# Two feed-forward layers: convolution biases and centre tap moved to ScalarE, five modulation vectors moved from TensorE to VectorE

## The chip, the cores and the metric

One core of one Trainium2 chip runs the whole program. The metric is the device time of one execution in microseconds; a kernel's time is the median of its runs. For the kernel before there are three runs: 2511.26, 2512.8 and 2514.46 us, median 2512.8 us. Engines are called as in the profile: PE is TensorE (PEld its weight loads), DVE is VectorE, ACT is ScalarE, POOL is GpSimd, SP is SyncE, whose queue issues the DMAs.

## The reference

Four transformer layers run one after the other on a latent stream `x` (512 tokens of 1024) and a context stream `ctx` (256 tokens): an attention layer with a feed-forward part (layer 0), an mLSTM layer with a feed-forward part (layer 1), and two gated mixing layers. Each layer is modulated by vectors that come from two conditioning inputs, `c` for the latents and `c_ctx` for the context. Cut to what the change touches:

```python
mod_lat = (jnp.dot(jax.nn.silu(c), ada_w[layer]) + ada_b[layer])[:, None, :]
mod_ctx = jnp.dot(jax.nn.silu(c_ctx), ada_w[layer]) + ada_b[layer]
sh1, sc1, gt1, sh2, sc2, gt2 = jnp.split(mod_lat, 6, axis=-1)
...
def dwconv(x, w, b):          # three taps along the tokens, zero padded at both ends of a stream
    ...
    return sum(xp[:, j:j + T] * w[j] for j in range(width)) + b

def conv_ffn(h, w_up, conv_w, conv_b, w_down):
    gate, val = jnp.split(jnp.dot(h, w_up), 2, axis=-1)
    return jnp.dot(jax.nn.silu(dwconv(gate, conv_w, conv_b)) * val, w_down)
```

In layer 1 the context is not updated any more after the mLSTM has read it, so `gt1`, `sc2`, `sh2` and `gt2` of layer 1 are needed for the latents alone, and so is the gate of the second mixing layer. The other vectors are needed for both streams.

## The kernel before, in words

Activations lie with channels on the partitions and tokens on the columns: 768 columns, context first (0 to 255), then latents (256 to 767). Two more columns, 768 and 769, carry the modulation shifts, so that a product's last two columns are the bias that each stream gets (latents, context). The normalisation factor of a token is applied after the product, as a row `h.r`.

Each fp32 product is made of three with the operands split into a high and a low part (`split`, line 355: ACT writes the high part, DVE the rest). Weights come by DMA from SP's queue into `raw` (three buffers) and are split into `wh` and `wl` (four half tiles each, `weight`, line 398) one weight ahead of the product that uses them. `lin` (line 407) issues a product into a PSUM tile from `A` (three of them in the feed-forward layers).

The work is one program order written by hand: `blk` (line 508) issues the splits for the next weight, the matmuls of a block, then `fill`, then `tick`, which runs what earlier blocks have put off with `later`; the evacuation of a block is so issued behind the matmuls of the next one. Every engine runs its own part of this order in sequence.

A feed-forward layer (`ffn`, line 896) goes through 22 groups of 128 hidden channels. A group has two products over eight tiles of inputs, gate and value, each 24 pairs of matmuls; in between the down products of earlier groups are issued (`plan_ffn`, line 875: chunks of 2, 2 and then six times 3 groups; for each of eight output tiles one product, evacuated by `add_x`, line 859). In layer 0 it covers both streams, in layer 1 the latents alone.

The gate's evacuation (`g1`, line 905) runs on DVE but for the two-column bias and the tanh: `put` (line 821) multiplies by `h.r` and adds the bias per stream, `conv` (line 842) makes the centre tap with the convolution's bias and then two taps per stream, `silu2` (line 852) the activation. The value's (`v1`, line 910) multiplies by the result and splits it for the down product.

Sixteen modulation vectors are made on the side (`modvec`, line 530). A vector takes eight steps. A step loads 128 rows of 1024 weights into an `ada` buffer (two of them, loads run two steps ahead) and issues four matmuls of 256 columns, one for each quarter of the columns (the profile counts each as two). After the last step ACT copies the result, PE transposes it twice, and DVE adds the bias (`turn`, line 550). `fill` (line 644) takes such steps off one list `todo`, in the order in which `run` (line 2332) put them there, as long as the `quota` of the stage lasts: 24 steps in the first layer's mixer, 48 in its feed-forward part, 24 in the second feed-forward part, 16 and again 16 in the first mixing layer. In a feed-forward layer `blk` takes one step per weight (two for groups 1 and 2), and the down products one for every second output tile. So the feed-forward part of layer 0 makes `gt2_0`, `sc1_1`, `sh1_1`, `gt1_1`, `sc2_1` and `sh2_1`; that of layer 1 `gt2_1`, `s_sc_0` and `s_sh_0`; `s_gt_1` comes last in the first mixing layer, two steps within its output products (line 2123) and six in the passage to the second (`fill(2)` in line 2153 and `pre`, line 2156).

Of the kernel before, what the change touches and what calls it, by code (L numbers as in the profile page):

```python
# [9 lines left out]
F32 = mybir.dt.float32  # L10
F32R = mybir.dt.float32r
BF16 = mybir.dt.bfloat16
AF = mybir.ActivationFunctionType
ALU = mybir.AluOpType
# [4 lines left out]
D = 1024  # L19
NL = 512  # L20
NC = 256
T = NL + NC
HALF = T // 2
W = 776
STATS = {0: (0,), 1: (1, 2), 2: (3, 4), 3: (5, 6), 4: (7,)}
CP = lambda j, qi, m: j == 1
KT = D // 128
FF = 2816
NFB = FF // 128
# [113 lines left out]
def _prepare(inp):  # L143

    a = {k: np.asarray(v) for k, v in inp.items()}
    o = dict(_constants())
    xt = np.concatenate([a["ctx"][0], a["x"][0]], 0).T
    o["xT"] = np.ascontiguousarray(xt.reshape(KT, 128, T))
    o["cT"] = np.ascontiguousarray(a["ctx_2"][0].T.reshape(KT, 128, NC))
    o["ada"] = a["ada_w"]  # L150
    o["mod"] = a["w_mod_2"]

    blk = lambda s, n: [np.arange(s + 128 * i, s + 128 * i + 128) for i in range(n)]
# [5 lines left out]
    for h in range(8):  # L159
        n, r = h * 96 + np.arange(64), h * 96 + 64 + np.arange(32)  # L160
# [19 lines left out]
    gt = np.concatenate([np.concatenate([g0 + s + np.arange(8), np.full(24, g0)]) for s in (0, 16, 8, 24)])  # L180
# [18 lines left out]
    cols, at = [], {}  # L199
# [30 lines left out]
    for n in ("gqa_q_g", "gqa_k_g"):  # L230
        g = a[n][0]
# [33 lines left out]
class _Kernel:  # L265


    def __init__(self, ctx, tc, I, at, out):
        self.tc, self.nc, self.I, self.at, self.out = tc, tc.nc, I, at, out
        pool = lambda name, bufs, **k: ctx.enter_context(tc.tile_pool(name=name, bufs=bufs, **k))  # L270
        self.kp = pool("k", 1)
        self.pa = pool("a", 36)
        self.pp = pool("pt", 3)
        self.pw = {n: pool(n, b) for n, b in (("raw", 3), ("ada", 2), ("wh", 4), ("wl", 4))}
        self.ps = pool("sm", 24)
        self.pr = pool("rm", 4)
        self.pm = pool("mo", 1)
        self.psa, self.banks = pool("psa", 2, space=PSUM), None
        self.dr = pool("dr", 1, space=DRAM)
        self.todo, self.due, self.mods, self.coming = [], [], {}, set()  # L280
        self.wq, self.wi, self.wraw, self.wsp = [], 0, {}, {}
        self.nraw = self.nspl = 0
        self.hook = self.mid = None
        self.quota, self.log = 0, False

    def split_psum(self, a, at=0):

# [229 lines left out]
    def cond(self, names, key):  # L517

        S = self.const("S" + key, [128, KT, 32])
        self.nc.vector.memset(S, 0.0)  # L520
        for v, n in enumerate(names):
            x = self.s(n, 0, KT)
            th = self.sm(8)
            self.act(th, x, AF.Tanh, scale=0.5)
            u = self.sm(8)
            self.ts(u, x, 0.5)
            self.stt(S[:, :, v], th, 1.0, u, ALU.add, ALU.mult)
        return S

    def modvec(self, name, S, w, c0, bias):  # L530
        nc = self.nc
# [319 lines left out]

    def silu2(self, x, c):

        th = self.a(name="th")
        self.act(th[:, c], x[:, c], AF.Tanh, scale=0.5)
        self.stt(x[:, c], th[:, c], 1.0, x[:, c], ALU.add, ALU.mult)
        return x
# [38 lines left out]
    def ffn(self, l, h, order, make_next):  # L896
        lat, c = h.lat, h.c
        segs = (SL,) if lat else (SL, SC)
        acts = {}
        nxt = None  # L900

        def gate(i):
            st = {}

            def g1(ps):
                g = self.put(ps, h)
                cv = self.conv(g, [self.s(f"fcw{l}{j}", i) for j in range(3)], self.s(f"fcb{l}", i), lat)
                st["s"] = self.silu2(cv, c)

            def v1(ps):  # L910
                v, cv = self.a(name="val"), st["s"]
                b = self.bias(ps)
                self.tt(v[:, c], ps[:, c], h.r[:, c])
                for s, (c0, c1) in enumerate(segs):
                    self.stt(v[:, c0:c1], v[:, c0:c1], b[:, s:s + 1], cv[:, c0:c1], ALU.add, ALU.mult)
                acts[i] = self.parts(v, c, "ah")
            seg = LATB if lat else ALLB
            if i == 0:
                self.begin([(f"w_up{l}", 0, seg, g1), (f"w_up{l}", 1, seg, v1)], h)
                return  # L920
            for j, evac in ((0, g1), (1, v1)):
                self.blk(f"w_up{l}", 2 * i + j, h.hs, seg, evac, 1 + (i < 3))

        def early(nxt):

            for k in range(KT):
                self.feed(nxt, k, True, (1,))
                if k:
                    yield
            self.sums(nxt, (1,))  # L930
            yield
            self.inverse(nxt, (1,))

        gt, gens = None, []
        step, _ = self.side(gens)
        for o in order:
            if o[0] == "up":
                gate(o[1])
                continue
            _, i, n, d0 = o  # L940
            last = i + n == NFB
            if gt is None:
                gt = self.half(f"gt2h_{l}", f"gt2_{l}")
            if last and not lat:
                self.tick()
                nxt = make_next()
            if lat and o is order[-2]:
                nxt = make_next()
                gens.append(early(nxt))
            xs = [acts.pop(j) for j in range(i, i + n)]  # L950
            b = WIDE[n]
            for m2 in range(D // b):
                w = self.weight(f"w_dn{l}", d0 + m2 * 128 * n * b)
                for e in range(b // 128):
                    ps = self.lin(w, xs, LAT if lat else ALL, off=128 * e, stride=b)
                    self.tick()
                    self.later(lambda m=b // 128 * m2 + e, ps=ps, n=nxt if last else None: self.add_x(m, ps, gt, lat, n))
                    step()
                    if e % 2:
                        self.fill(1)  # L960
        self.flush()
        return nxt

    def project(self, name, xs, segs, gt, lat, nxt):
# [1367 lines left out]
    def run(self):  # L2332
        nc, I = self.nc, self.I
# [8 lines left out]
        nc.vector.memset(self.eps, EPS)  # L2342
        S1 = self.cond(("c", "c_ctx"), "1")
        S2 = self.cond(("c_2", "c_ctx_2"), "2")
        for l in range(2):
            for j, n in ((1, "sc1"), (0, "sh1"), (2, "gt1"), (4, "sc2"), (3, "sh2"), (5, "gt2")):
                if l or j > 1:
                    self.modvec(f"{n}_{l}", S1, I["ada"][l], 1024 * j, self.s(f"ada_b{l}", 8 * j, 8))
        for l in range(2):
            for j, n in ((1, "s_sc"), (0, "s_sh"), (2, "s_gt")):  # L2350
                self.modvec(f"{n}_{l}", S2, I["mod"][l], 1024 * j, self.s(f"mod_b{l}", 8 * j, 8))
        self.plan_even()
        orders = [self.plan_ffn(0)]
        self.plan_odd()
# [29 lines left out]
        def norm(A, g, sc, sh, lat=False):  # L2384
            return lambda: self.start(self.gain(A, sc, g), self.mod(sh), lat)

        h = self.start(self.const("A_a0", [128, KT, 2]), self.const("m_sh1_0", [128, KT, 2]))
        pre = self.first_mods(S1, I["ada"][0], 1024, 0, self.s("ada_b0", 8, 8), self.s("ada_b0", 0, 8), self.s("n1g0", 0, KT), h, consts, after)
        self.quota = 24
        h = self.even(h, pre, norm("f0", self.s("n2g0", 0, KT), "sc2_0", "sh2_0"))  # L2390
        self.quota = 48
        h = self.ffn(0, h, orders[0], norm("a1", self.s("n1g1", 0, KT), "sc1_1", "sh1_1"))
        h = self.odd(h, norm("f1", self.s("n2g1", 0, KT), "sc2_1", "sh2_1", True))
        self.quota = 24
        h = self.ffn(1, h, orders[1], norm("s0", self.s("gpre0", 0, KT), "s_sc_0", "s_sh_0"))
        self.quota = 16
        h, pre, post = self.second(0, h, norm("s1", self.s("gpre1", 0, KT), "s_sc_1", "s_sh_1"))
# [25 lines left out]
```

## Time and profile before

| | before |
|---|---|
| median of 3 runs | 2512.8 us |
| the profiled execution's own time | 2511.48 us |
| its span in the trace | 2509.7 us |
| mean granted TensorE clock | 0.989 of full speed |
| PE busy | 2441.3 us, 97% |
| DVE busy | 1554.0 us, 62% |
| ACT busy | 962.2 us, 38% |
| POOL busy | 213.9 us, 9% |
| DMA | 234.99 MB, mean 94 GB/s |

The profiled execution took 1.8 us more than its span; this lies around the span and is taken as fixed. Busy shares are averages over stages: PE does most of the work nearly everywhere, and what a stage costs is read from the stage. A timeline line that ends in "xN" is N instructions of one kind in a row, its duration from the start of the first to the end of the last. The feed-forward part of layer 0 lies at about 507 to 1104 us of the span, that of layer 1 at about 1434 to 1813 us, the passage between the mixing layers at about 2203 to 2266 us.

### The profile page before, as it was taken

The page shows a single profiled execution, that of the slowest core. Times are in us where ns is not written, and L with a number is a line of the kernel's source. Part 1 is how long each engine was busy: PE and PEld are TensorE (multiplying, and loading weights), DVE is VectorE, ACT ScalarE, POOL GpSimd, SP SyncE. Part 2 cuts the span into 40 slices and gives each one's busy share as a digit, 9 for nine tenths or more (in the row PEclk, how much of TensorE's full clock was granted, in tenths as well). Part 3 has the DMA queues.
Part 4 walks back from the last instruction along what each step waited for, and adds up shares of the span by engine and source line. Part 5 has one row for each costly group of instructions (what it writes and reads, how often), then busy time and mean ns, then how long its engine had stood idle before and what let it go on. Part 6 is the DMA issues. An engine that isn't in the chain of part 4 may idle for free.

```text
span 2509.7 us, 40462 instructions
## 1 busy us (share of the span) xinstructions
PE 2441.3 (97%) x16296; PEld 2038.9 (81%) x16296; DVE 1554.0 (62%) x2780; ACT 962.2 (38%) x2203; POOL 213.9 (9%) x149
## 2 busy tenths in 40 slices
PE   7998999999999999998999999999999999999998
PEld 5776666887888888887889888999978778879797
DVE  4436876556555656668566566766755575267764
ACT  4226666322211222243445422233432374343563
POOL 2001232100000000022110100000010000130001
PEclk9999999999999999998999999999999999999999
DMA  8441110124343321113122255222223202332012
GB/s 286 152 153 46 32 65 29 61 91 143 117 128 126 110 84 68 55 64 110 60 64 68 93 175 178 97 97 93 85 82 121 90 1 69 102 118 78 18 47 88
DMA packets 81866, 234.99 MB, mean 94 GB/s; under 512 B 9936, under 2 KB 22288, under 8 KB 81680
## 3 DMA queue, kind: packets, MB, share of 16 engines
q1 hardware_dynamic: 81392, 232.36, 28.1%
q8 instruction: 128, 2.10, 0.3%
q14 instruction: 58, 0.48, 0.1%
q10 hardware_dynamic: 288, 0.07, 0.0%
HBM read 229.73 MB, written 2.66 MB: 93 GB/s over the span
## 4 chain that ended last, share of the span: by engine, by line
PE 86%; DVE 7%; ACT 3%; DMA 2%; issue 1%; SPq 0%; POOL 0%; DVEq 0%; ACTq 0%; POOLq 0%
PE A L353 69%; PE B L353 14%; PE B L1075 3%; DMA ada<-in_ada_dram 1%; DVE sm L1064 1%; DVE wl L344 1%; DVE kf L344 1%; DVE conv L341 1%; ACT P L332 0%; DVE hl L341 0%; DVE put L344 0%; ACT wh L332 0%; DMA stsel<-in_stat_dram 0%; ACT hh L332 0%; DVE y L344 0%
## 5 line engine op out<-in xcount | busy, mean ns | idle before, releaser
L353 PE MATMUL A<-hh,wh 128*128 128x258 f32 (+2 forms) x2704 | 648.0, 321 | 11.9 <-ACT wh L332 4.1
L353 PE MATMUL A<-hl,wh 128*128 128x258 f32 (+2 forms) x2704 | 631.9, 315 | 2.7 <-DVE hl L341 2.7
L353 PE MATMUL A<-hh,wl 128*128 128x258 f32 (+2 forms) x2704 | 631.5, 315 | 0.1
L344 DVE TENSOR_TENSOR wl<-raw,wh 128x512 fp32r<-128x512 f32 (+2 forms) x533 | 368.8, 714 | 414.3 <-ACT wh L332 400.7
L332 ACT ACTIVATE wh<-raw 128x512 fp32r<-128x512 f32 (+2 forms) x533 | 310.7, 603 | 566.7 <-PE A L353 398.5
L353 PEld LDWEIGHTS A<-hh,wh 128*128 128x128 f32 x2704 | 420.2, 191 | 73.7 <-issue 12.1
L353 PEld LDWEIGHTS A<-hl,wh 128*128 128x128 f32 x2704 | 420.0, 190 | 36.3 <-DVE hl L341 3.8
L353 PEld LDWEIGHTS A<-hh,wl 128*128 128x128 f32 x2704 | 420.1, 190 | 33.8 <-DVE wl L344 0.5
L344 POOL TENSOR_TENSOR sq<-sq 128x768 f32<-128x768 f32 (+2 forms) x45 | 65.5, 1457 | 1200.6 <-ACT sq L332 595.9
L332 ACT ACTIVATE P<-A,sm 128x768 f32<-128x768 f32 (+3 forms) x176 | 128.0, 727 | 96.9 <-DVE sm L1064 90.9
L353 PE MATMUL A<-ah,wh 128*128 128x512 f32 (+1 forms) x528 | 163.1, 363 | 1.2 <-DVE x L341 1.1
L353 PE MATMUL A<-ah,wl 128*128 128x512 f32 (+1 forms) x528 | 159.7, 357 | 0.0
L353 PE MATMUL A<-ahl,wh 128*128 128x512 f32 (+1 forms) x528 | 159.3, 356 | 0.0
L1064 DVE TENSOR_REDUCE sm<-A 128x1 f32<-128x768 f32 (+3 forms) x176 | 129.2, 735 | 44.4 <-PE A L353 43.6
L341 DVE SCALAR_TENSOR_TENSOR x<-A,gt2h,x 128x512 f32<-128x512 f32 x192 | 119.7, 656 | 43.3 <-PE A L353 43.2
L1075 PE MATMUL B<-ident,P 128*128 128x128 f32 x768 | 124.4, 286 | 7.7 <-DVE pt L1078 2.7
L1075 PEld LDWEIGHTS B<-ident,P 128*128 128x128 f32 x768 | 83.8, 143 | 51.2 <-issue 21.5
L332 ACT ACTIVATE th<-conv 128x768 f32<-128x768 f32 (+1 forms) x52 | 38.4, 738 | 223.1 <-DVE conv L341 223.1
L341 DVE SCALAR_TENSOR_TENSOR conv<-put,small,conv 128x511 f32<-128x511 f32 (+1 forms) x168 | 111.5, 678 | 5.0
L353 PEld LDWEIGHTS A<-ah,wh 128*128 128x128 f32 x528 | 86.8, 188 | 27.0 <-issue 4.6
L344 DVE TENSOR_TENSOR put<-A,rbc 128x768 f32<-128x768 f32 (+1 forms) x111 | 93.2, 840 | 21.4 <-ACT sm L332 21.4
L353 PE MATMUL B<-ada,S 128*32 128x256 f32 x1152 | 91.2, 397 | 8.7 <-DMA ada<-in_ada_dram 8.5
(369 smaller groups left out, 3301.1 us busy)
## 6 DMA issues: line engine op xcount, KB each, us to landing
raw<-in_w_up_dram SPq DMA_DIRECT2D x88, 512.0 KB, 3.3
raw<-in_w_in_dram SPq DMA_DIRECT2D x81, 512.0 KB, 4.5
ada<-in_ada_dram SPq DMA_DIRECT2D x80, 512.0 KB, 4.1
ada<-in_mod_dram SPq DMA_DIRECT2D x48, 512.0 KB, 3.8
raw<-in_w_dn_dram SPq DMA_DIRECT2D x48, 384.0 KB, 3.1
raw<-in_w_o_dram SPq DMA_DIRECT2D x24, 512.0 KB, 4.3
ada<-in_ada_dram SPq DMA_DIRECT2D x16, 384.0 KB, 8.0
raw<-in_w_dn_dram SPq DMA_DIRECT2D x8, 512.0 KB, 5.7
```

The source lines that it names most:

```text
L332: return self.nc.scalar.activation(out, in_, f, **k)
L341: return self.nc.vector.scalar_tensor_tensor(out, x, sc, y, op0=op0, op1=op1)
L344: return (e or self.nc.vector).tensor_tensor(out, x, y, op=op)
L353: return self.nc.tensor.matmul(out, l, r, start=start, stop=stop)
L1064: nc.vector.tensor_reduce(g.nm[:, z], u.ps[:, cols], axis=AX.X, op=ALU.max, negate=True)
L1075: nc.tensor.transpose(ps[:, 128 * i:128 * i + 128], u.P[:, c:c + 128], self.ident)
```

## The change

Three things are changed.

In the feed-forward gate the biases leave the streams. The gate is kept without its bias, in a buffer with one column of padding on either side of a stream; ACT writes minus the bias there, DVE multiplies PSUM by `h.r` once per stream, ACT makes the centre tap with a bias that stands for both (`bc`, one two-column DVE operation with the sum of the taps, `wsum`), and DVE adds the two outer taps in one operation each over both streams at once.

Five vectors, those needed for the latents alone, are made by `modrow` in place of `modvec`. Their weights come transposed (`lone`): a step loads a tile of 128 output channels by 1024 and multiplies it by the conditioning row, held on all partitions, with the sum as a second output of the same DVE instruction. The row is written to DRAM once for each of the two conditioning inputs and loaded by one DMA on all 128 partitions, once in each feed-forward layer.

The order of the list and one quota change: the feed-forward part of layer 0 now takes 56 steps (24 of `modvec`, then 32 of `modrow`), that of layer 1 two vectors of `modvec` and then `s_gt_1` by `modrow`.

```diff
@@ _prepare
+    o["lone"] = np.stack([w[:, 1024 * j:1024 * j + 1024].T.reshape(KT, 128, D)
+                          for w, j in [(a["ada_w"][1], j) for j in (2, 4, 3, 5)] + [(a["w_mod_2"][1], 2)]])
@@ _Kernel
+    def modrow(self, name, v, i, bias):
+        nc, st = self.nc, {}
+
+        def load(k):
+            st[k] = self.pw["ada"].tile([128, 1024], F32, tag="ada", name="ada")
+            nc.sync.dma_start(st[k], self.I["lone"][i, k])
+
+        def step(k):
+            if self.row is None or self.row[0] != v:
+                self.row = v, self.pt(n=D)
+                nc.sync.dma_start(self.row[1], self.sd[v:v + 1].to_broadcast([128, D]))
+            if k == 0:
+                st["m"] = self.const("m_" + name, [128, KT, 2])
+                nc.gpsimd.memset(st["m"], 0.0)
+            m, raw = st["m"], st.pop(k)
+            nc.vector.scalar_tensor_tensor(raw, raw, 1.0, self.row[1], op0=ALU.mult, op1=ALU.mult, accum_out=m[:, k, 0:1])
+            if k == KT - 1:
+                self.tt(m[:, :, 0], m[:, :, 0], bias, ALU.add)
+                self.mods[name] = m
+
+        for k in range(KT):
+            self.todo.append((lambda k=k: load(k), lambda k=k: step(k)))
@@ silu2
-        th = self.a(name="th")
+        th = self.a(n=W, name="th")
@@ ffn, gate
             def g1(ps):
-                g = self.put(ps, h)
-                cv = self.conv(g, [self.s(f"fcw{l}{j}", i) for j in range(3)], self.s(f"fcb{l}", i), lat)
-                st["s"] = self.silu2(cv, c)
+                w = [self.s(f"fcw{l}{j}", i) for j in range(3)]
+                g, d, bc = self.a(n=W, name="gate"), self.a(n=W, name="conv"), self.sm()
+                self.ts(bc, ps[:, T:T + 2], wsum[:, i:i + 1], self.s(f"fcb{l}", i), ALU.mult, ALU.add)
+                for v, ((c0, c1), z) in enumerate(zip(segs, at)):
+                    n = c1 - c0
+                    self.act(g[:, z - 1:z + n + 1:n + 1], ps[:, T + v:T + v + 1].to_broadcast([128, 2]), scale=-1.0)
+                for v, ((c0, c1), z) in enumerate(zip(segs, at)):
+                    n = c1 - c0
+                    self.tt(g[:, z:z + n], ps[:, c0:c1], h.r[:, c0:c1])
+                    z0 = z - 2 if len(segs) > v + 1 else z
+                    self.act(d[:, z0:z + n], g[:, z0:z + n], AF.Identity, scale=w[1], bias=bc[:, v:v + 1])
+                for j in (0, 2):
+                    self.stt(d[:, lo:hi], g[:, lo - 1 + j:hi - 1 + j], w[j], d[:, lo:hi])
+                st["s"] = self.silu2(d, slice(lo, hi))
...
+        wsum = self.const("wsum", [128, NFB])
+        self.tt(wsum, self.s(f"fcw{l}0", 0, NFB), self.s(f"fcw{l}1", 0, NFB), ALU.add)
+        self.tt(wsum, wsum, self.s(f"fcw{l}2", 0, NFB), ALU.add)
+
+        at = (NC,) if lat else (NC + 3, 1)
+        lo, hi = at[-1], at[0] + NL
...
         self.flush()
+        self.row = None
         return nxt
@@ run
+        for n, l, j in (("gt1", 0, 2), ("sc2", 0, 4), ("sh2", 0, 3), ("gt2", 0, 5), ("sc1", 1, 1), ("sh1", 1, 0)):
+            vec(n, l, j)
+        for i, (n, j) in enumerate((("gt1", 2), ("sc2", 4), ("sh2", 3), ("gt2", 5))):
+            self.modrow(n + "_1", 0, i, self.s("ada_b1", 8 * j, 8))
+        vec2("sc", 0, 1)
+        vec2("sh", 0, 0)
+        self.modrow("s_gt_1", 1, 4, self.s("mod_b1", 16, 8))
+        for n, l, j in (("gt", 0, 2), ("sc", 1, 1), ("sh", 1, 0)):
+            vec2(n, l, j)
+        self.sd = self.dr.tile([2, D], F32, tag="sd", name="sd")
...
         h = self.even(h, pre, norm("f0", self.s("n2g0", 0, KT), "sc2_0", "sh2_0"))
-        self.quota = 48
+        for v, S in enumerate((S1, S2)):
+            nc.sync.dma_start(self.sd[v].rearrange("(k p) -> p k", p=128), S[:, :, 0])
+        self.quota = 56
```

## Rows read from the trace of the kernel before

**Rows 1.** Page, part 1: busy us, share of the span, instructions.

```profile
PE 2441.3 (97%) x16296; PEld 2038.9 (81%) x16296; DVE 1554.0 (62%) x2780; ACT 962.2 (38%) x2203; POOL 213.9 (9%) x149
```

**Rows 2.** Busy time in stretches: PE, PEld, DVE, ACT, POOL, clock, DMA.

```profile
689.00:886.00 197.00, 197.00 (x1209) 160.27 (x1209) 111.31 (x185) 39.91 (x77) 0.00 (x0) 1.00 0.39 125
886.00:1083.00 197.00, 197.00 (x1125) 172.52 (x1125) 123.90 (x203) 44.05 (x86) 0.00 (x0) 1.00 0.19 64
...
1563.00:1813.00 250.00, 250.00 (x1763) 234.21 (x1765) 176.77 (x291) 81.48 (x182) 6.09 (x6) 1.00 0.28 93
```

**Rows 3.** Chain in order of time, layer 0 feed-forward, with steps: start, us, what.

```profile
652.15 8.62 PE A L353 x48
...
661.34 8.62 PE A L353 x48
...
688.92 0.37 PE B L553 x2
...
698.29 6.50 PE A L353 x36
...
705.36 6.50 PE A L353 x36
```

**Rows 4.** Timeline of PE, layer 0, no steps: two pairs, 24 pairs apart.

```profile
895.91 0.51 PE L353 MATMUL A<-hh,wh 128*128 128x512 f32 x2
...
904.33 0.51 PE L353 MATMUL A<-hh,wh 128*128 128x512 f32 x2
```

**Rows 5.** Chain in order of time, layer 1 feed-forward, with steps.

```profile
1537.61 5.93 PE A L353 x48
...
1544.11 5.93 PE A L353 x48
```

**Rows 6.** Timeline of PE, layer 1, no steps: two pairs, 24 pairs apart.

```profile
1659.75 0.41 PE L353 MATMUL A<-hl,wh 128*128 128x256 f32 x2
...
1665.50 0.41 PE L353 MATMUL A<-hl,wh 128*128 128x256 f32 x2
```

**Rows 7.** Timeline of PE and of DVE around the passage between the mixing layers.

```profile
2212.55 1.07 PE L353 MATMUL B<-ada,S 128*32 128x256 f32 x16
2213.55 1.16 PE L353 MATMUL B<-rm,ident 128*128 128x128 f32 x8
2217.60 0.79 PE L353 MATMUL A<-hh,wh 128*128 128x256 f32 x2 [2.89 <-ACT hh L332]
...
2211.82 0.29 DVE L341 SCALAR_TENSOR_TENSOR rm<-rm 128x128 f32<-128x128 f32 x1
```

**Rows 8.** Groups by shape: count, busy us, mean ns of one, idle before.

```profile
L341 DVE SCALAR_TENSOR_TENSOR conv<-th,conv 128x768 f32<-128x768 f32 x28 | 26.8, 957 | 21.8 <-ACT th L332 21.8
...
L332 ACT ACTIVATION_READ_ACCUMULATOR P<-A,sm 128x1 f32 x176 | 34.2, 194 | 0.0
```

**Rows 9.** Timeline of DVE, layer 1, no steps: a gate, then a value.

```profile
1666.08 0.69 DVE L344 TENSOR_TENSOR put<-A,rbc 128x512 f32<-128x512 f32 x1
...
1667.90 1.54 DVE L341 SCALAR_TENSOR_TENSOR conv<-put,small,conv 128x511 f32<-128x511 f32 x2
1670.14 0.69 DVE L341 SCALAR_TENSOR_TENSOR conv<-th,conv 128x512 f32<-128x512 f32 x1 [0.70 <-ACT th L332]
1670.75 1.16 DVE L344 TENSOR_TENSOR wl<-raw,wh 128x512 fp32r<-128x512 f32 x2
...
1674.60 0.74 DVE L341 SCALAR_TENSOR_TENSOR x<-A,gt2h,x 128x512 f32<-128x512 f32 x1
```

**Rows 10.** Timeline of DVE and of PE, layer 1, second set of down products.

```profile
1521.00 2.06 DVE L341 SCALAR_TENSOR_TENSOR x<-A,gt2h,x 128x512 f32<-128x512 f32 x3
...
1521.80 0.49 PE L353 MATMUL A<-ah,wh 128*128 128x512 f32 x1 [0.60 <-DVE x L341]
```

**Rows 11.** DMA issues: engine, count, KB each, median us to landing.

```profile
pt<-cb SPq DMA_DIRECT2D x16, 256.0 KB, 5.0
...
de<-de SPq DMA_DIRECT2D x4, 4.0 KB, 7.5
```

More of the change, by code (lines that the diff above doesn't have):

```diff
@@ L283, in __init__ @@
         self.hook = self.mid = None
-        self.quota, self.log = 0, False
+        self.quota, self.log, self.row = 0, False, None
     def split_psum(self, a, at=0):
@@ L913, in v1 @@
                 self.tt(v[:, c], ps[:, c], h.r[:, c])
-                for s, (c0, c1) in enumerate(segs):
-                    self.stt(v[:, c0:c1], v[:, c0:c1], b[:, s:s + 1], cv[:, c0:c1], ALU.add, ALU.mult)
+                for s, ((c0, c1), z) in enumerate(zip(segs, at)):
+                    self.stt(v[:, c0:c1], v[:, c0:c1], b[:, s:s + 1], cv[:, z:z + c1 - c0], ALU.add, ALU.mult)
                 acts[i] = self.parts(v, c, "ah")
@@ L2344, in run @@
         S2 = self.cond(("c_2", "c_ctx_2"), "2")
[L2345 to L2351, printed above, removed]
+        vec = lambda n, l, j: self.modvec(f"{n}_{l}", S1, I["ada"][l], 1024 * j, self.s(f"ada_b{l}", 8 * j, 8))
+        vec2 = lambda n, l, j: self.modvec(f"s_{n}_{l}", S2, I["mod"][l], 1024 * j, self.s(f"mod_b{l}", 8 * j, 8))
+        for n, l, j in (("gt1", 0, 2), ("sc2", 0, 4), ("sh2", 0, 3), ("gt2", 0, 5), ("sc1", 1, 1), ("sh1", 1, 0)):
[8 more added lines that the diff above has]
+        self.sd = self.dr.tile([2, D], F32, tag="sd", name="sd")
         self.plan_even()
```

## The prediction

> **What bounds the kernel now.** I read the page first: PE is busy 97% of the span, DVE 62%, ACT 38% [rows 1]. An average over stages proves little, so I went to the stretches in which the change acts. In the feed-forward part of layer 0, with modulation steps (689 to 886 us) and without them (886 to 1083 us), PE is busy all 197.00 of 197 us, and in that of layer 1 without steps 250.00 of 250 us [rows 2]. So nothing hides the steps there: each microsecond of PE taken out shortens the run, as long as DVE, which takes the work over, does not become late. DVE is busy 123.90 of 197 us (63%) in layer 0 and 176.77 of 250 us (71%) in layer 1 where no steps run [rows 2].
>
> **What one step costs PE.** A block of 24 matmul pairs starts every 661.34 - 652.15 = 9.19 us with a step in it [rows 3]; the same 24 pairs without one take 904.33 - 895.91 = 8.42 us [rows 4]. The step costs 0.77 us, more than its own matmuls' place in the chain, since the pairs at either side of it move apart. In the down products 18 pairs with a step take 705.36 - 698.29 = 7.07 us [rows 3] against 18/24 x 8.42 = 6.32 us: 0.75. I use 0.76. In layer 1 a block takes 1544.11 - 1537.61 = 6.50 us with a step [rows 5] and 1665.50 - 1659.75 = 5.75 us without [rows 6]: 0.75. The two transposes that end a vector take 0.37 us in the chain [rows 3], partly in place of the gap behind a step; I take 0.2.
>
> **Part 1: five vectors leave PE.** The list decides where. Layer 0's feed-forward part loses `gt1_1`, `sc2_1`, `sh2_1`: 24 x 0.76 + 3 x 0.2 = 18.8 us. Layer 1's loses one vector in sum (`gt2_1` has been made before, `s_gt_1` comes in as a row product): 8 x 0.75 + 0.2 = 6.2 us. In the first mixing layer the eight steps of `s_gt_1` go. Two lie among full products: 2 x 0.76 = 1.5 us. Two stand together at 2212.55 and hold up the products that spread the normalisation row by 2213.55 - 2212.55 = 1.0 us; DVE had finished that row at 2211.82 + 0.29 = 2212.11, so this 1.0 us is gained. The other four lie where PE waits anyway (2.89 us for ACT at the first product [rows 7]): nothing. With the transposes: 2.7 us. Together 27.7 us.
>
> **Part 2: forty row products arrive on DVE.** The trace has no such operation with a sum output. Its nearest rows are the same instruction with two SBUF inputs and no sum: 957 ns for 768 columns [rows 8] and 0.69 us for 512 [rows 9], so (957 - 690)/256 = 1.04 ns a column and 0.16 us fixed. For 1024 columns this gives 1.22 us, the low bound. A sum that is read out costs ACT 194 ns [rows 8]; I take 1.4 us, since the instruction itself is known and only the read-out is new. The high bound is two cycles for each column: 0.16 + 1024 x 2.08 ns + 0.19 = 2.5 us.
>
> Layer 0: a block takes PE 8.42 us. DVE's 63% of it is 5.3 us; a row product makes 6.7; DVE's existing waits for ACT (21.8 us over 28 activations [rows 8], twice in two blocks) add 0.8: 7.5 us. It fits, so this is costed at nothing under PE; if DVE ran 1 us over per block instead, 32 steps would cost up to 32 us.
>
> Layer 1 is tighter. In two blocks PE has 11.5 us; DVE's gate runs from 1666.08 to 1670.75 = 4.67 us, the splits and the value's evacuation to 1674.60 = 3.85 us, the other block's splits 1.2 us [rows 9]: 9.7 us. Two row products make 12.5 us, 1.0 us too much, for two groups only; `A` has three tiles and weights are split a block ahead, so an arrear of 2 us is carried. But four of the eight row products fall into down products with short blocks. There two output tiles take PE 12 x 5.75/24 = 2.9 us, and DVE 2 x 0.69 (three evacuations in 2.06 us [rows 10]) + half of 1.16 (a split pair serves four tiles [rows 9]) + 1.4 = 3.4 us. PE already waits 0.60 us for such an evacuation there [rows 10]. So I give these four steps back whole: -3.0 us. Bounds for layer 1: 6.2 us if the arrear is carried, -3 us if a late row load is added.
>
> **Part 3: the gate.** Per gate DVE loses the bias additions and the centre tap (in layer 1 between 1666.08 + 0.69 and 1667.90, 1.13 us [rows 9]) and in layer 0 two of four outer taps; it gains a two-column operation (0.2 us) and a wait for ACT's centre tap, which I size by the tanh of the same shape, 0.70 us of idle time [rows 9]. In layer 1 the gate stays at 4.67 - 1.13 + 0.2 + 0.7 = 4.4 us; in layer 0 it gets shorter, with two streams overlapping ACT and DVE. ACT's additions fall on an engine that is busy 81.48 of 250 us [rows 2]. Behind the waiting DVE stand the next weight's low parts, for which PE waits one block later. As PE does not wait for the gate now, part 3 gains and costs nothing; uncovered it could cost what the wait exceeds the margin of 11.5 - 9.7 = 1.8 us.
>
> **Part 4: queues.** The 40 weight loads replace 40 of the same 512 KB on SP's queue; their buffers are now freed by DVE. New are two scattered writes of 1024 runs of 4 bytes and two loads of a row onto 128 partitions. The nearest rows: four scattered loads of 256 runs each, together 1024 runs in flight, land in 7.5 us, and a 256 KB broadcast in 5.0 us [rows 11]. Two writes, about 15 us, stand in front of weight loads when two weights, 2 x 8.42 = 16.8 us of PE, are in hand: 0, at worst 15 if that cover failed. The broadcast keeps DVE waiting 0 to 5 us at the first row product of each layer, with evacuations and splits behind it; in layer 0 a block of slack covers it, in layer 1 it is in the bound above. I take 0.
>
> **Sum.** 18.8 + (6.2 - 3.0) + 2.7 = 24.7 us. The profiled execution, 2511.48 us (span 2509.7 and 1.8 around it), lies 1.3 us under the median of 2512.8; it becomes 2486.8, the median 2488.1. I forecast 2487.5 us, with 2482 to 2493 for this case alone. About 0.2% (5 us) is what a measurement of this kernel can tell from no change.
>
> **Rivals.** *Row products at half rate.* Each then takes 2.5 us. For it: a sum output is new here. Against it: without it the same instruction with two fp32 SBUF inputs runs at 1.04 ns a column, one a cycle like a plain product. In layer 0 a block would ask DVE for 5.3 + 2.5 + 0.8 = 8.6 us of 8.42: some 0.2 x 32 = 6 us, of which the shorter gate gives 1 to 2 back. In layer 1 eight times 1.1 us more, of which some 2 us are carried: 7 us. Time 2487.5 + 4.5 + 7 = 2499 us. Chance 0.16. [...]
>
> *The hand-over to ACT becomes the bound, and the kernel gets slower.* The place is the first outer tap of each of the 22 gates of layer 1, where DVE's queue stops until ACT has run the centre tap. With a wait of 0.7 us there are 1.8 us of margin and 0.3 gained; it loses once the wait passes 2.8 us, and at 3.9 us the loss, 22 x 1.1 = 24 us, cancels the gain. At 4.2 us: 22 x 1.4 = 31 us, 2487.5 + 31 = 2518.5 us. For it: ACT runs in order and splits weights too. Against: ACT idles two thirds of that stretch [rows 2] and the tanh hand-over costs 0.70 us. Chance 0.04.
>
> *The saving is eaten.* DVE's arrears in layer 0, or the scattered writes, take 15 to 25 us back: about 2508. Against it stands DVE's 63%. Chance 0.05.
>
> *More is gained.* The four steps in layer 1's down products come free too and the passage shortens further: 2487.5 - 3.0 - 2.5 = 2482 and below. Chance 0.09.
>
> **Chances and range.** The forecast case has 0.66. Faster by over 0.2% (under 2507.8): 0.66 + 0.16 + 0.09 = 0.91, less 0.02 for the eaten saving's doubtful edge: 0.89. Within 0.2%: 0.07. Slower: 0.04. The range of 2481 to 2500 takes in the forecast, half rate and most of the better case.
>
> **What would show it.** Right: in layer 0 blocks of 8.42 us from 689 us on with PE busy throughout; row products of about 1.4 us; layer 1's up blocks 5.75 us with row products beside them, while its second down products gain nothing; the passage's spread products about 1 us earlier. Wrong: row products of 2.5 us; waits of PE for `wl` or for evacuations in the stretches where it had none; idle time of DVE before the outer taps above 2.8 us; weight loads landing late at the start of layer 0's feed-forward part.

## The result and the profile after

The changed kernel takes 2487.23 us (median of 4 runs, 2485.67 to 2489.86) beside 2512.03 us for the kernel before (4 runs): ratio 0.9903, 95% interval 0.9892 to 0.9915. The forecast was 2487.5 us. The profiled execution took 2486.04 us, with a span of 2484.3 us, 25.4 us less than before.

The page's busy time by engine, after:

```profile
PE 2408.3 (97%) x15966; PEld 2027.6 (82%) x15966; DVE 1549.1 (62%) x2771; ACT 1010.7 (41%) x2286; POOL 215.9 (9%) x154
```

Against [rows 1], PE is 33 us less busy and ACT 48 us more. DVE stands where it was (1549.1 us for 1554.0): the gate gave up 45.5 us (e1, below) and forty row products take 51.8. The same stretches as in [rows 2] (columns: PE, PEld, DVE, ACT, POOL, granted clock, DMA share, GB/s):

```profile
689.00:886.00 197.00, 197.00 (x1124) 172.24 (x1123) 141.24 (x235) 53.65 (x107) 0.00 (x0) 1.00 0.39 137
886.00:1083.00 197.00, 197.00 (x1126) 172.45 (x1125) 125.30 (x197) 63.41 (x127) 7.75 (x4) 1.00 0.23 77
1563.00:1813.00 250.00, 247.47 (x1739) 229.83 (x1738) 164.86 (x273) 99.27 (x206) 11.52 (x10) 1.00 0.30 92
```

In the first stretch DVE now has 141 us of 197 to do in place of 111, and PE still never stops. The 2.53 us that PE lacks in the last one are 0.28 us of waiting and the 2.24 us in front of the next layer, which now begins inside that stretch, at 1812.40. The chain of waits in the first stretch, in order of time (start, us, what):

```profile
678.59 0.57 PE B L356 x8
679.16 8.63 PE A L356 x48
687.79 0.22 PE B L581 x2
688.01 202.14 PE A L356 x1151
```

Up to 687.79 it has the steps of [rows 3]; then all pieces in between are gone, and PE's products run on with no wait.

**Where the time came from.** Four marks in PE's timeline cut the span: the statistics products at the start of layer 0's feed-forward part, the first product behind its last down product, the same two for layer 1. Before:

```profile
524.35 0.86 PE L353 MATMUL B<-sq,stsel 128*32 128x192 f32 x16
1103.47 0.59 PE L353 MATMUL A<-hh,wh 128*128 128x512 f32 x2 [0.20 <-DVE hl L344]
1445.52 0.65 PE L353 MATMUL B<-sq,stsel 128*32 128x128 f32 x16
1834.25 0.59 PE L353 MATMUL A<-hh,wh 128*128 128x512 f32 x2 [2.25 <-DVE x L341]
```

After, with the products that spread the row in the passage as a fifth mark (before: 2213.55 [rows 7]):

```profile
523.78 0.86 PE L356 MATMUL B<-sq,stsel 128*32 128x192 f32 x16
1083.96 0.59 PE L356 MATMUL A<-hh,wh 128*128 128x512 f32 x2 [0.20 <-DVE hl L347]
1426.13 0.65 PE L356 MATMUL B<-sq,stsel 128*32 128x128 f32 x16
1812.40 0.67 PE L356 MATMUL A<-hh,wh 128*128 128x512 f32 x2 [2.24 <-DVE x L344]
2189.10 1.05 PE L356 MATMUL B<-rm,ident 128*128 128x128 f32 x8
```

| stretch | before | after | gained | predicted |
|---|---|---|---|---|
| layer 0, feed forward | 579.12 | 560.18 | 18.94 | 18.8 |
| mLSTM | 342.05 | 342.17 | -0.12 | 0 |
| layer 1, feed forward | 388.73 | 386.27 | 2.46 | 3.2 |
| first mixing layer to the mark in the passage | 379.30 | 376.70 | 2.60 | 2.7 |

What is left of the 25.4 us lies ahead of the first mark (0.57 us) and behind the last (0.95 us), where the change does little; the stretch behind the last mark lasts 295.2 to 296.5 us in the change and in e2 to e12 below, among which nothing there differs.

**The row product** by shape (count, busy us, mean ns of one, idle before it):

```profile
L550 DVE SCALAR_TENSOR_TENSOR ada<-ada,pt 128x1024 f32<-128x1024 f32 x40 | 48.6, 1216 | 4.6 <-DMA pt<-sd 4.0 <-issue 0.6
L550 DVE DVE_READ_ACCUMULATOR ada<-ada,pt 128x1 f32 x40 | 3.2, 81 | 0.0
```

1.216 us is the low bound of the prediction (1.22, from [rows 8, 9]) and the read-out is an instruction of its own, 0.08 us; taken together 1.30 us where 1.4 was taken and 2.5 feared.

**The gate** by shape, layer 0 and layer 1, then ACT's centre tap in layer 1:

```profile
L344 DVE SCALAR_TENSOR_TENSOR conv<-gate,small,conv 128x770 f32<-128x770 f32 x44 | 44.9, 1021 | 23.8 <-ACT conv L335 23.1
L344 DVE SCALAR_TENSOR_TENSOR conv<-gate,small,conv 128x512 f32<-128x512 f32 x44 | 33.1, 752 | 20.2 <-ACT conv L335 19.4
L335 ACT ACTIVATE conv<-gate,sm,small 128x512 f32<-128x512 f32 x22 | 17.9, 816 | 16.7 <-DVE gate L347 16.7
```

DVE waits 23.1/22 = 1.05 us a gate in layer 0 and 19.4/22 = 0.88 us in layer 1 for the centre tap, where 0.7 was sized: the tap takes ACT 0.82 us, the tanh of the same shape 0.63 us. There is a second wait that the prediction left out: DVE's product stands behind the bias columns that ACT writes into the same buffer, 7.8 us in 22 gates of layer 1. So a gate of layer 1 keeps DVE from 1544.47 to 1549.46 us, 4.99 us with its waits, where it took 4.67 before and 4.4 was forecast, although DVE has less work in it.

**Layer 1 while its row products run.** PE's waits over that part, after:

```profile
PE A L356 <- DVE x L344: 3.8, 6, 1.3
PE A L356 <- DVE val L347: 1.2, 1, 1.2
PE B L356 <- DMA ada<-in_mod_dram: 0.2, 1, 0.2
```

(us in total, times, longest.) Before, there were two waits for `x`, 1.1 us. Two of the waits one by one:

```profile
1504.90 0.50 PE L356 MATMUL A<-ah,wh 128*128 128x512 f32 x1 [0.81 <-DVE x L344]
1551.14 0.50 PE L356 MATMUL A<-ah,wh 128*128 128x512 f32 x1 [1.17 <-DVE val L347]
```

The second comes 17 us behind the last row product (1533.20 us). DVE's timeline at the first of the two:

```profile
1501.63 0.74 DVE L344 SCALAR_TENSOR_TENSOR x<-A,gt2h,x 128x512 f32<-128x512 f32 x1
1502.94 1.23 DVE L550 SCALAR_TENSOR_TENSOR ada<-ada,pt 128x1024 f32<-128x1024 f32 x1 [0.57 <-issue]
1504.10 0.08 DVE L550 DVE_READ_ACCUMULATOR ada<-ada,pt 128x1 f32 x1
1504.10 1.41 DVE L344 SCALAR_TENSOR_TENSOR x<-A,gt2h,x 128x512 f32<-128x512 f32 x2
1505.42 1.22 DVE L550 SCALAR_TENSOR_TENSOR ada<-ada,pt 128x1024 f32<-128x1024 f32 x1
```

and the chain there:

```profile
1497.41 4.23 DMA pt<-sd
1501.71 0.67 DVE x L344
1502.43 1.68 PE A L356 x6
```

Row products alternate with two evacuations each, and the first of them starts behind a row load that began at 1497.41; DVE is busy for most of that load and idles 0.57 us in front of the product. So there were two suspects for what layer 1 lost: DVE's work, as predicted, and the late row.

### The profile page after: what moved, and what is told of

Its sections match the earlier page's. It is cut to its first block, busy times and chain, and to the rows that moved or that the text cites. A ratio compares the mean times of both kernels' runs of the same rounds, so it can differ in the third digit from the quotient of the medians.

```text
span 2484.3 us, 39893 instructions
## 1 busy us (share of the span) xinstructions
PE 2408.3 (97%) x15966; PEld 2027.6 (82%) x15966; DVE 1549.1 (62%) x2771; ACT 1010.7 (41%) x2286; POOL 215.9 (9%) x154
## 4 chain that ended last, share of the span: by engine, by line
PE 85%; DVE 8%; ACT 3%; DMA 2%; issue 1%; SPq 0%; POOL 0%; DVEq 0%; ACTq 0%; POOLq 0%
PE A L356 68%; PE B L356 13%; PE B L1124 3%; DVE wl L347 1%; DMA ada<-in_ada_dram 1%; DVE conv L344 1%; DVE sm L1113 1%; DVE kf L347 1%; ACT P L335 0%; DVE x L344 0%; ACT wh L335 0%; DVE put L347 0%; ACT hh L335 0%; DMA stsel<-in_stat_dram 0%; DVE hl L344 0%
## 5 line engine op out<-in xcount | busy, mean ns | idle before, releaser
L344 DVE SCALAR_TENSOR_TENSOR conv<-gate,small,conv 128x770 f32<-128x770 f32 (+1 forms) x88 | 78.0, 886 | 44.1 <-ACT conv L335 42.5
L356 PEld LDWEIGHTS A<-ah,wl 128*128 128x128 f32 x528 | 86.8, 188 | 15.6
L356 PEld LDWEIGHTS A<-ahl,wh 128*128 128x128 f32 x528 | 87.0, 188 | 14.4
L1127 DVE COPY pt<-B 128x384 f32<-128x384 f32 (+1 forms) x128 | 66.5, 520 | 46.5 <-PE B L1124 32.1
```

What stands on the lines that cost most here:

```text
L344: return self.nc.vector.scalar_tensor_tensor(out, x, sc, y, op0=op0, op1=op1)
L356: return self.nc.tensor.matmul(out, l, r, start=start, stop=stop)
L1127: nc.vector.tensor_copy(d, src)
```

## The experiments

All times are medians, with the ratio to the kernel before on the same chip. The last columns are the lengths of the two feed-forward parts between the marks above, in the profiled run.

| run | us | ratio, 95% interval | layer 0 | layer 1 |
|---|---|---|---|---|
| before | 2512.03 | 1 | 579.12 | 388.73 |
| the change | 2487.23 | 0.9903 (0.9892 to 0.9915) | 560.18 | 386.27 |
| e1, gate only | 2509.64 | 0.9989 (0.9980 to 0.9998) | 579.14 | 387.48 |
| e2, rows only | 2488.23 | 0.9903 (0.9889 to 0.9917) | 560.22 | 386.75 |
| e8, row early | 2485.61 | 0.9897 (0.9880 to 0.9914) | 560.19 | 385.34 |
| e4, short rows | 2481.29 | 0.9877 (0.9862 to 0.9891) | 560.19 | 382.15 |
| e5, all rows in layer 0 | 2482.16 | 0.9875 (0.9861 to 0.9889) | 560.24 | 382.18 |
| e11, the same, gate of before | 2484.36 | 0.9887 (0.9872 to 0.9902) | 560.15 | 383.20 |
| e3, rows twice | 2502.50 | 0.9961 (0.9947 to 0.9975) | 566.94 | 394.22 |
| e6, centre tap twice | 2497.91 | 0.9944 (0.9929 to 0.9958) | 564.83 | 394.25 |
| e7, centre tap four times | 2567.27 | 1.0216 (1.0201 to 1.0231) | 606.65 | 423.08 |
| e9, two streams | 2484.71 | 0.9890 (0.9874 to 0.9907) | 559.48 | 382.17 |
| e10, the same, gate of before | 2482.78 | 0.9880 (0.9865 to 0.9895) | 559.28 | 383.20 |
| e12, writes four times | 2494.22 | 0.9928 (0.9911 to 0.9944) | 568.59 | 386.11 |

The lengths of the two parts tell more than the totals, since a stretch in which nothing was edited moves the total: the mLSTM part lasts 338.21 us in the profiled run of e5 and 343.78 us in that of e2, with the granted clock in its first 100 us at 0.95 and 0.90.

### Which half of the change gains

**e1, the gate alone** on the kernel before:

```diff
-                g = self.put(ps, h)
-                cv = self.conv(g, [self.s(f"fcw{l}{j}", i) for j in range(3)], self.s(f"fcb{l}", i), lat)
-                st["s"] = self.silu2(cv, c)
...
+                    self.act(d[:, z0:z + n], g[:, z0:z + n], AF.Identity, scale=w[1], bias=bc[:, v:v + 1])
+                for j in (0, 2):
+                    self.stt(d[:, lo:hi], g[:, lo - 1 + j:hi - 1 + j], w[j], d[:, lo:hi])
+                st["s"] = self.silu2(d, slice(lo, hi))
```

> Only the gate is changed; all sixteen vectors are made on PE as before. Theory (DVE and ACT have room, PE never waits for the gate): same as the kernel before, 2512 us within 2.5 us, although DVE's busy time falls by some 40 to 60 us. Rival (the relief of DVE in the gate is itself part of the gain): 2507 us or less. Rival (the hand-over to ACT in the gate costs): 2517 us or more.

Measured: 2509.64 us. DVE is 45.5 us less busy than before (1508.5 against 1554.0), and layer 0's part is as long as before to 0.02 us; layer 1's is 1.25 us shorter. The theory holds: 45 us taken off an engine for which PE hardly waits bring 0.1%.

**e2, the row products alone**: the changed kernel with the lines of the diff above taken back, so with the gate of before:

> Only the row products, with the gate as before. Theory (in layer 0 a block then asks DVE for 5.3 + 1.3 + 0.8 = 7.4 us of the 8.42 us that PE needs, and in layer 1 only a few blocks are short): 2487 to 2490 us, so nearly the whole gain stands without the new gate. Rival (the new gate makes the room that the row products need): layer 0 gives back 0.2 us or more for each of 32 steps, 2494 us or more.

Measured: 2488.23 us, the same ratio as the change. The whole gain is the row products'; the new gate is not what makes room for them. e11 says it once more: with all rows in layer 0, DVE in the stretch from 689 to 886 us is busy 141.19 us with the new gate and 151.36 us with the old one, and PE 197.00 us in both.

```profile
689.00:886.00 197.00, 197.00 (x1124) 172.24 (x1123) 151.36 (x255) 41.82 (x83) 0.00 (x0) 1.00 0.39 137
```

(e11 is e5, below, with the same lines taken back.)

> All five row vectors in layer 0 as in that run, with the gate of the kernel before. Theory (the gate plays no part while DVE has room): 2482 us within 2.5 us. Rival (the new gate is what makes the room): 2487 us or more.

Measured: 2484.36 us, as the theory has it. In all four pairs of runs that differ in the gate alone the new one shortens layer 1's part a little (1.25, 0.48, 1.02 and 1.03 us) and layer 0's never by more than 0.1 us. Why layer 1 gains that microsecond is open: PE's waits for DVE there are no fewer with the new gate (1.7 us in e5, 1.8 us in e11). Beside row products the gain is the smallest, 0.48 us: there PE's wait for `val` is 1.17 us with the new gate and 0.37 us with the old one (e2), so in that pair the waits for ACT seem to cost something.

### What layer 1 gave back

**e8, the row loaded at the fourth group**:

```diff
+            if i == 3:
+                self.row = l, self.pt(n=D)
+                self.nc.sync.dma_start(self.row[1], self.sd[l:l + 1].to_broadcast([128, D]))
```

> As the change, but each layer's row is loaded at its fourth group, long before the first row product needs it. If the late row load (DVE stands 4.2 us for it in layer 1) is what layer 1 loses by: 2484 us. If the row products beside the short blocks of the down products are (the prediction's reason): 2486.5 to 2487.5 us. Layer 0 is expected to stay as it is in both cases.

Measured: 2485.61 us; layer 1's part is 0.93 us shorter. By the medians alone this is unclear; by the part, the late row is the smaller share. The 4.2 us in the expectation is the time that the row was on its way, not a wait of DVE, which idles the 0.57 us above. In layer 0 DVE does stand 4.0 us for its row, and PE never waits for it.

**e4, row products over 8 columns**:

```diff
-            nc.vector.scalar_tensor_tensor(raw, raw, 1.0, self.row[1], op0=ALU.mult, op1=ALU.mult, accum_out=m[:, k, 0:1])
+            nc.vector.scalar_tensor_tensor(raw[:, :8], raw[:, :8], 1.0, self.row[1][:, :8], op0=ALU.mult, op1=ALU.mult, accum_out=m[:, k, 0:1])
```

> The row products cover 8 of the 1024 columns (most of the sum is left out), with all loads and the order as in the change. Theory (the 32 of layer 0 lie wholly under PE, the eight of layer 1 cost the 2.8 us that an earlier row load does not give back): layer 0's part as long as with the change, 560.0 us, layer 1's some 3 us shorter, 2484 us. Rival (the products cost something in layer 0 too): layer 0's part below 558 us and the time below 2481 us. Rival (loads and queues cost it, not the products): 2487 us.

Measured: 2481.29 us. A row product is down from 1.30 to 0.24 us. Layer 0's part stays at 560.19 us, so the 32 row products there cost nothing at all. Layer 1's becomes 4.12 us shorter, and its waits for DVE are down to

```profile
PE A L356 <- DVE x L344: 1.9, 3, 1.2
```

where there were seven waits of 5.0 us. Loads, queues and the late row are as in the change in this run, so it is DVE's time in the row products that layer 1 paid with: it gains 2.46 us when they are there, and 388.73 - 382.15 = 6.58 us when they are not. Of the 6.58 us about 1 us is the new gate's; with the old gate and no row product (e11) it is 388.73 - 383.20 = 5.53 us. The late row matters only in so far as DVE is late afterwards.

**e5, all five in layer 0**, a version that should then beat the change:

```diff
+        self.modrow("s_gt_1", 1, 4, self.s("mod_b1", 16, 8))
         vec2("sc", 0, 1)
         vec2("sh", 0, 0)
-        self.modrow("s_gt_1", 1, 4, self.s("mod_b1", 16, 8))
...
-        self.quota = 56
+        self.quota = 64
...
-        self.quota = 24
+        self.quota = 16
```

> All five row vectors are made in the feed-forward part of layer 0 (64 steps there), layer 1 keeps 16 steps on PE and no row product. Theory (the 3.7 us by which layer 1 fell short of its 6.2 us come from DVE being late there, and layer 0 has room for eight more): layer 1's part then shortens by 6.2 us instead of 2.5 us and layer 0's stays, 2483.5 us. Rival (the eight products only move their cost to layer 0): 2487 us as with the change.

Measured: 2482.16 us, ratio 0.9875 (0.9861 to 0.9889), under the change's interval. Layer 1's part is 382.18 us, as if its row products were free (e4), and layer 0's 560.24 us, with eight more in it. PE's waits for DVE in layer 1's part:

```profile
PE A L356 <- DVE x L344: 1.7, 3, 1.3
```

### How much room DVE has

**e3, each row product twice**, the half-rate rival made by hand:

```diff
             nc.vector.scalar_tensor_tensor(raw, raw, 1.0, self.row[1], op0=ALU.mult, op1=ALU.mult, accum_out=m[:, k, 0:1])
+            nc.vector.scalar_tensor_tensor(raw, raw, 1.0, self.row[1], op0=ALU.mult, op1=ALU.mult, accum_out=m[:, k, 1:2])
```

> Each row product is issued twice (the second sum goes to a column that no later work reads), 2 x 1.30 = 2.6 us a step, as the prediction's half-rate rival would have had it (2.5 us). By the rival's sum layer 0 then asks DVE for 8.7 us of PE's 8.42 us a block and gives back 4 to 9 us, layer 1 gives back about 7 us more: 2495 to 2503 us. If DVE has more slack than the prediction counted: 2491 us or less.

Measured: 2502.50 us, 15 us over the change. Layer 0 gives back 6.8 us and layer 1 7.95 us. So the rival's sum was near (6 less 1 to 2, and 7), and this instruction simply doesn't run at half rate here (1216 ns, above).

**e9, two more vectors with two row products a step**, and **e10**, the same with the gate of before:

```diff
+            if two:
+                nc.vector.scalar_tensor_tensor(self.row2[1], raw, 1.0, self.row2[0], op0=ALU.mult, op1=ALU.mult, accum_out=m[:, k, 1:2])
...
-        for n, l, j in (("gt1", 0, 2), ("sc2", 0, 4), ("sh2", 0, 3), ("gt2", 0, 5), ("sc1", 1, 1), ("sh1", 1, 0)):
+        for n, l, j in (("gt1", 0, 2), ("sc2", 0, 4), ("sh2", 0, 3), ("gt2", 0, 5)):
             vec(n, l, j)
+        self.modrow("sc1_1", 0, 5, self.s("ada_b1", 8, 8), True)
+        self.modrow("sh1_1", 0, 6, self.s("ada_b1", 0, 8), True)
```

> As the run with all five row vectors in layer 0 (2482.2 us), and two vectors that both streams need, sc1_1 and sh1_1, made there by two row products a step as well. Theory: 16 steps and two turns leave PE, 16 x 0.76 + 0.4 = 12.6 us, and a step of two row products gives back what each step of the doubled run did, 6.8 / 32 = 0.21 us, 16 x 0.21 = 3.4 us: 2473 us. Rival (the first half of layer 0's part has less room, since its blocks follow one another with a step of two products each): half or less of it, 2477 us or more.

> As the run before it with the gate of the kernel before. Where DVE is the engine that comes late, the gate's DVE time should show at last. Theory: the 16 steps of two products lose some 0.5 us each more than with the new gate, 2 to 10 us slower than that run. Rival (the wait for ACT in the new gate takes what it saves): within 2 us of it.

Measured: 2484.71 and 2482.78 us, no faster than e5; my expectation of 2473 us missed by nearly all of its gain. Layer 0's part is 559.48 us, 0.76 us shorter where 9.2 were expected. A stretch of e9 in which the double products run:

```profile
600.00:640.00 40.00, 36.07 (x195) 30.80 (x193) 33.09 (x55) 10.98 (x22) 0.00 (x0) 0.96 0.28 96
```

PE's waits for DVE in layer 0's part, in e9 and then in e10:

```profile
PE A L356 <- DVE x L344: 5.7, 3, 2.8
PE A L356 <- DVE val L347: 1.6, 1, 1.6
```

```profile
PE A L356 <- DVE x L344: 8.0, 5, 2.5
PE A L356 <- DVE val L347: 1.7, 1, 1.7
```

DVE is busy 33.09 of 40 us and PE only 36.07: PE now waits for DVE. The 0.21 us a step that I took from e3 did not carry over, though e3's double products follow one another as closely (one in 6.9 us there, one in 6.7 us here). PE waits 7.3 us for DVE in layer 0's part of e9 and 5.1 us in that of e3, and in e9 the granted clock falls as well, to 0.86 from 570 to 580 us and to 0.83 from 630 to 640 us; over layer 0's part of e3 it is 1.00. Why these 16 steps cost more than those 32 was not taken apart.

With the old gate PE waits 9.7 us for DVE in place of 7.3, so the gate's DVE time does show, if by less than the second expectation's theory had it; but in that trace the clock stays at 1.00, and the part comes out as long (559.28 us). So the equal lengths don't show that the gate's time plays no part: in these two traces a longer wait in the one stands beside a lower clock in the other. In the medians the expected 2 to 10 us do not appear.

### The hand-over to ACT

**e6 and e7, the centre tap two and four times** (`range(4)` in e7):

```diff
-                    self.act(d[:, z0:z + n], g[:, z0:z + n], AF.Identity, scale=w[1], bias=bc[:, v:v + 1])
+                    for _ in range(2):
+                        self.act(d[:, z0:z + n], g[:, z0:z + n], AF.Identity, scale=w[1], bias=bc[:, v:v + 1])
```

> ACT runs each centre tap twice, so the wait of DVE in the gate of layer 1 grows from 0.9 us by the tap's 0.82 us to 1.7 us. By the prediction's margin (it loses once the wait passes 2.8 us) nothing is lost: 2487 us. If the margin is smaller, or the weight halves that ACT splits come late for PE: 2491 us or more.

Measured: 2497.91 us, 10.7 us over the change, where nothing was expected: layer 0 loses 4.65 us, layer 1 7.98 us. Two stretches of layer 1 in e6, with the last row products in the first and none in the second:

```profile
1534.00:1584.00 50.00, 45.40 (x301) 40.81 (x301) 33.91 (x55) 19.02 (x36) 0.00 (x0) 1.00 0.43 137
1584.00:1634.00 50.00, 50.00 (x353) 46.80 (x352) 32.62 (x52) 20.06 (x38) 0.00 (x0) 1.00 0.31 95
```

and PE's three longest sums of waits over layer 1's part:

```profile
PE A L356 <- DVE x L344: 5.1, 7, 1.4
PE A L356 <- ACT wh L335: 2.0, 2, 1.4
PE A L356 <- DVE val L347: 2.0, 1, 2.0
```

Where no steps run, PE is busy all 50.00 us: there the margin stands. Most of the loss lies where modulation steps and row products have already spent it, and part of it behind ACT, whose weight halves come late for PE (2.0 us). In layer 0 PE's longest wait, 2.38 us, is for ACT's copy at the end of a vector, which stands behind the taps in ACT's queue; in the change it is 0.50 us.

> ACT runs each centre tap four times, so the wait in the gate of layer 1 grows to 0.9 + 3 x 0.82 = 3.4 us, past the 2.8 us of the prediction's slower rival: 22 x 0.6 = 13 us lost, 2500 us, most of it in layer 1's part, with PE waiting there for DVE. If three tiles of A and weights split ahead carry such a wait: 2490 us or less. If ACT becomes the bound in layer 0 as well (1.4 us for both streams four times): layer 0's part longer than 562 us.

Measured: 2567.27 us, slower than before. DVE's waits for the centre tap in layer 1's part, then a stretch there without steps:

```profile
DVE conv L344 <- ACT conv L335: 75.5, 22, 3.4
```

```profile
1690.00:1840.00 150.00, 144.53 (x1049) 136.59 (x1048) 87.50 (x140) 70.86 (x127) 0.00 (x0) 0.98 0.27 85
```

The wait is 75.5/22 = 3.43 us, as worked out (3.4). In that stretch PE idles 5.47 us in 150, some 0.4 us in the 11.5 us of a gate, near the 0.6 of the expectation; with steps, and in layer 0 (46.5 us lost, which the third sentence allowed for), far more. So the threshold of 2.8 us is about right for steady blocks, and too high by at least a microsecond for the part as a whole.

### The scattered writes

**e12, the two writes four times**:

```diff
-        for v, S in enumerate((S1, S2)):
-            nc.sync.dma_start(self.sd[v].rearrange("(k p) -> p k", p=128), S[:, :, 0])
+        for v, S in enumerate((S1, S2) * 4):
+            nc.sync.dma_start(self.sd[v % 2].rearrange("(k p) -> p k", p=128), S[:, :, 0])
```

SP's queue in the change, then in e12 (start, us, what; the duration runs from the first write's start to the last one's end), what SP waited for there, and PE:

```profile
483.21 1.04 SPq L2446 DMA_DIRECT2D sd<-S  x2
491.23 9.04 SPq L384 DMA_DIRECT2D raw<-in_w_up_dram  x2
```

```profile
486.57 32.94 SPq L2446 DMA_DIRECT2D sd<-S  x8
519.57 5.15 SPq L384 DMA_DIRECT2D raw<-in_w_up_dram  x3
...
SPq L2446 <- DMA sd<-S: 28.1, 5, 10.6
...
534.58 1.01 PE L356 MATMUL A<-hh,wh 128*128 128x512 f32 x2 [6.57 <-ACT wh L335]
...
520.00:560.00 40.00, 33.43 (x215) 27.57 (x214) 15.16 (x24) 10.97 (x23) 0.00 (x0) 0.91 0.44 96
```

> The two scattered writes of the conditioning rows are issued four times, 8 x 1024 runs of 4 bytes ahead of the weight loads of layer 0's feed-forward part; the pair landed in 12.3 us with the change. Theory (they are covered only by the two weights that PE has in hand, 16.8 us): four pairs one after the other take 49 us, PE waits for weights at the start of that part and 20 to 32 us are lost, 2507 to 2519 us. Rival (they run beside the weight loads and hold up nothing): 2487 us.

Measured: 2494.22 us; layer 0's part is 8.41 us longer. Neither theory hits the size. SP does stand in the writes for 32.94 us, 28.1 us of it waiting for the writes themselves: each rewrite of a row waits until the write before it has landed. That is three landings one after the other and not four, since SP goes on once the last pair is issued. The next weight load starts 33.00 us behind the first write, in the change 8.02 us behind it (SP waits there for a free `raw` buffer anyway), so it is 24.98 us late; PE waits 6.57 of these, and the weights in hand cover 18.4, near the 16.8 of the expectation. A single pair, as in the change, holds SP for 1.04 us, less than the wait for the buffer, and PE waits for no weight there: nothing lost. (e9's three writes to three rows hold SP for 3.23 us.)

## Why the prediction was right, and where it was off

The total came out within 0.3 us, and some of that is luck: layer 1's term is 0.7 us too high, 1.5 us of the gain lies outside the marks and in no term, and the median of the kernel before moved from 2512.8 us (three runs) to 2512.03 us (four). The terms of layer 0 and of the first mixing layer are right by themselves.

- **Price of a step and part 1.** 18.8 us forecast for layer 0, 18.94 measured; 2.7 us for the mixing layer, 2.60 measured. In the passage DVE's row now ends at 2188.75 and the spread products begin 0.35 us later, where it was 1.44 us: 1.09 us for the 1.0 forecast.
- **Row products in layer 0 free.** Shown: e4 cuts them to 0.24 us each and the part stays as long to 0.01 us; e5 adds eight at no cost.
- **Layer 1 gives back.** Right in kind, but 2.46 us were gained for 3.2 forecast (6.2 less 3.0), and both terms are off. Taking out the eight steps gains 5.53 us (e11: old gate, no row product), not 6.2: at the second set of down products PE now waits 1.27 us for DVE where it waited 0.60 us [rows 10], so the step taken out there in part only lengthened a wait. The new gate adds 1 us, sized at nothing. The row products take back 4.1 us (e4) for the 3.0 taken, and not only at the short down products: of the waits that go with them in e4, 0.81 and 0.63 us stand there, and 1.17 us for `val` (an up block's result) and 0.50 us come later, at 1551 and 1554 us. So the term for the down products was too high, and the arrears in the up blocks, which the prediction said are carried, are not; the late row adds up to 0.9 us (e8), which stood only in the bound.
- **Cost of a row product.** 1.30 us for 1.4. The read-out was sized by ACT's 194 ns and takes DVE 81 ns. The half-rate rival is refuted as a fact of the instruction: 1216 ns for 1024 columns is the rate of the rows without a sum (1.22 us [rows 8, 9]). As a price it was good (2499 us forecast, 2502.5 us when made by hand). The prediction's cycle is the 1.04 ns a column of those rows; twice that with a sum was the author's assumption. Here the instruction is no slower with a sum than without, nor with two SBUF sources (0.69 us for 512 columns [rows 9]) than with one of them in PSUM (0.74 us, `x` above).
- **The gate.** "Gains and costs nothing" holds for layer 0; in layer 1 it gains some 1 us, and 0.48 us beside row products. The forecast of 4.4 us for DVE's gate in layer 1 was short mainly by the wait for ACT's bias columns: it measures 4.99 us. e1, e2 and e11 show that the gate isn't what the gain rests on.
- **The slower rival.** Its mechanism is real (e7 makes the kernel slower than before), its threshold was wrong for the part as a whole: the margin of 1.8 us was read from a stretch without steps, and the wait decides first where steps and row products stand. At 1.7 us of wait, a microsecond under the threshold, 10.7 us are lost (e6), part of it because ACT's own work comes late for PE (2.38 us for a copy in layer 0, 2.0 us for weight halves in layer 1). The chance of 0.04 hung on a margin that was thinner than it said; the measured wait of 0.88 us stayed below it.
- **Queues.** The writes were taken at 0 and cost 0: SP's queue stands in them for 1.04 us and PE waits for no weight behind them; they land in 12.3 us, for an estimate of 15. The load of the row costs nothing in layer 0 and up to 0.9 us in layer 1 (e8).

## What to carry to other kernels

Work moved off the bounding engine gained its full price only where the engine that took it had room in that very stretch: the same row product costs nothing beside layer 0's blocks of 8.4 us and about half a microsecond in layer 1 (4.1 us for eight), where blocks are shorter, so choose the stretch before tuning the engine. Read a margin where the new work will stand, not in the quiet stretch next to it, and add up all that is to draw on it: the 1.8 us read in layer 1 without steps did not keep e6, at 1.7 us of wait, from losing 7.98 us in that layer. Relieving an engine for which the bounding one hardly waits gained next to nothing here: 45.5 us less of DVE's busy time brought 0.1% (e1).

## What the runs showed of the hardware

- In the change each of the 40 DVE instructions with a sum as second output (1216 ns) is followed by a separate read of the accumulator, 81 ns, also 40 times; at the one shown above the next instruction's start is the read's own start in the trace (1504.10 for both).
- A wait of PE cost more than its own length in two places. In e12 PE waited 6.57 us and the part grew by 8.41 us; the granted clock of the 40 us around the wait was 0.91, where the change has PE busy throughout at 1.00. In e9 the clock was 0.86 and 0.83 in two stretches of 10 us, at waits of 2.76 and 1.84 us; in e10, with waits of 2.49 and 1.84 us, it stayed at 1.00, so not every such wait stood beside a lower clock. At 1.00 too, in layer 1, PE waits 3.1 us more in the change than in e4 and the part is 4.12 us longer.
- Two scattered writes of 1024 runs each stand in SP's queue for 1.04 us, three to three different rows for 3.23 us (e9). Eight that rewrite two rows take 32.94 us, 28.1 us of which SP waits for earlier writes to land (e12).
